# Who makes the low parts of the expert weights: every other subtraction on GpSimd, and no raw products

## The chip, the cores and the metric

The kernel runs on one NeuronCore of a Trainium2 chip, as one launch. The metric is the device time in microseconds (us), the median of several runs. The engines named below are TensorE (PE in the profile; PEld is its weight load), VectorE (DVE), ScalarE (ACT), GpSimd (POOL) and SyncE (SP, which issues most of the transfers).

## What is computed

A trunk of two layers over 256 latent tokens and 256 context tokens of width 1024: modulated norms, attention of four kinds, and in each layer a feed-forward block with 16384 experts. The change touches only that block. For a block of tokens the reference does

```
q = (xb @ wq).reshape(128, 8, 2, 128)
s = einsum('thpd,pnd->thpn', q, sub_keys)
sv, si = top_k(s, 16)
...
a = einsum('thkd,td->thk', u[eidx], xb)
wgt = gelu(a) * softmax(fv)
out = einsum('thk,thkd->td', wgt, v[eidx])
```

Each token chooses 16 of 16384 experts for each of 8 heads, from two lists of 128 keys. Layer 0 does it for 512 tokens, layer 1 for 256.

## The kernel before

Instead of gathering the chosen experts' rows, the kernel multiplies all experts for most tokens (three blocks of 128 tokens in layer 0, both blocks in layer 1; the fourth block of layer 0 is gathered). The 16384 experts are 128 chunks of 128. For a chunk i, the *first product* (`achunk`, L1032) is the chunk's 128 rows of `u` against all tokens, in PSUM; ScalarE applies Gelu and evicts it into a ring (L1046). The *second product* (`fchunk`, L1188) multiplies the gated result by the chunk's rows of `v` and is accumulated over all chunks.

Products are made to nearly full precision in a fast matmul type: an operand is split into a high part (a ScalarE cast, L169) and a low part (operand minus high part, a VectorE subtraction, L170; both in `split`, L168), and `mm3` (L191) makes three matmuls of each product: high by high (L193) and the two mixed ones (L194, L195). The names in the profile: `w` is a raw weight tile (six buffers), `ws` a split half (six buffers, so three chunks), `hh`/`hl`/`hp` the split activations. A first product of a chunk has 8 blocks of the depth, so 24 matmuls: high by high (L193), high by the activations' low part (L194), low by high (L195). In `achunk` the weight's low part is first needed by the third matmul, the call at L195.

Layer 1 has a second way: for every fifth of its first chunks (`raw(i)`, L1023: i below the lag, i % 5 == 0) the unsplit weights go against unsplit activations `h32` at the slow matmul type (`product8`, L212, matmul L215: 8 matmuls that the trace shows as 16 passes). Such a chunk needs no cast and no subtraction. `RAWQ` does the same for some blocks of layer 1's query projection and is not touched.

The stretch in question: while routing (top-16 lists, VectorE) and gates are worked out, TensorE has no second products to make, so the kernel runs ahead with first products: 27 chunks in layer 0, 47 in layer 1 (`LAG`), which lie in the ring. The order is written by the program: `prologue()` (L1059) yields after each piece of routing or gate work, and whenever its accumulated weight allows, the loop at L1082 emits the next `achunk`. In the gates (`gates`, L928) VectorE makes one-hot tables (`oh`, L954: 128x2048 fp16) and products with the gate (`og`, L957, L960), ScalarE scales a part (L964), TensorE multiplies them (L978), ScalarE evicts (L981). In layer 0 a filler also does the conditioning of later layers (`ada`, L252, with a GpSimd memset at L241).

`achunk(i)` first asks for loads of chunks i to i+3 on SP's queue (`load_u`), then for splits of i and i+1 (`split_u`, L1026), then emits the matmuls and Gelu. An instruction waits on its engine in program order: a cast of chunk i+1 needs the ws buffers of chunk i-2 to be free (its matmuls done), the subtraction needs the cast, TensorE's matmuls need both. After the lag the same `achunk` runs in the main loop, with the second products; there all splits stay on VectorE and ScalarE.

GpSimd in this kernel: the small power functions of the norms (L317), and in layer 0's main loop the copies of gather indices (L1135, L1138) and the gathers (L1141).

Of the kernel before, what the change touches and what calls it, by code (L numbers as in the profile page):

```python
# [10 lines left out]
F = mybir.dt.float32  # L11
# [5 lines left out]
OP = mybir.AluOpType  # L17
# [26 lines left out]
RSTEP = 4  # L44
U_AHEAD = (1, 3)
RAWQ = (3, 6, 9, 12, 15)
RAWU = (1, 5)
CAND = ((0, 1, 16, 0), (1, 3, 8, 16), (4, 4, 4, 40), (8, 8, 1, 56))
CAND_LO = (0, 16, 24, 32, 40, 44, 48, 52, 56, 57, 58, 59, 60, 61, 62, 63)

# [41 lines left out]
class Kernel:  # L92
# [903 lines left out]
    def peer(self, l, xs, sq, nd):  # L996

        nc = self.nc
# [3 lines left out]
        lag = LAG[l]  # L1002
# [12 lines left out]
        ustr, usp, useen, vstr, gstr, ring = {}, {}, set(), {}, {}, {}  # L1015

        def load_u(i):
            if i < NCH and i not in useen:
                useen.add(i)
                ustr[i] = self.wraw_t()  # L1020
                nc.sync.dma_start(ustr[i], A["uT"][l, i].rearrange("p k e -> p (k e)"))

        def raw(i):  # L1023
            return self.h32 is not None and i < lag and i % RAWU[1] < RAWU[0]

        def split_u(i):  # L1026
            if i < NCH and i not in usp and not raw(i):
                h, o = self.wsp_t(), self.wsp_t()
                self.split(ustr.pop(i), h, o)
                usp[i] = (h, o)  # L1030

        def achunk(i):  # L1032
            for k in range(U_AHEAD[1] + 1):
                load_u(i + k)
            for k in range(U_AHEAD[0] + 1):
                split_u(i + k)
            p = self.ps()
            if raw(i):
                self.product8(p[:, c], ustr.pop(i))
            else:  # L1040
                uh, ul = usp.pop(i)
                for k in range(8):
                    b = slice(k * 128, (k + 1) * 128)
                    self.mm3(p[:, c], uh[:, b], ul[:, b], hh[:, k, c], hl[:, k, c], k == 0, k == 7)
            ring[i] = rg.t("ring", [128, TD])
            nc.scalar.activation(ring[i], p[:, c], AF.Gelu)  # L1046

        def ahead(b):
            if b >= 14:
                load_u(b - 14)  # L1050
            if b == 17:
                split_u(0)
# [26 lines left out]
        i = 0  # L1079
        tot = (6 - EARLY[l]) * RW0[l] + 6 * (nd - 1) * RW + nd * (32 + 2 * GPIPE)  # L1080
        done = 0
        for n, w in enumerate(prologue()):  # L1082
            done += w
            if n % FSTEP == 0:
                next(filler, None)
            while i < lag and i * tot < done * (lag - TAIL[l]):
                achunk(i)
                i += 1
# [121 lines left out]
        while i < lag:  # L1210
            achunk(i)
            i += 1
        split_v(0)
        weight(0)
        for j in range(NCH):
            load_v(j + 2)
            if j + lag < NCH:
                achunk(j + lag)
            split_v(j + 1)
            weight(j + 1)  # L1220
            if lt and j < LATE:
                next(lt, None)
            elif lt:
                n1 = pace(j)
                for n in range(nu, n1):
                    use(n)
                gather(nu + NGB, n1 + NGB, wts[j + 1][:, 0, 0:1].bitcast(F) if j + 1 < NCH else None)
                nu = n1
            if j < NCH - 2:
                fchunk([j])  # L1230
# [264 lines left out]
```

## Time and profile before

| what | us |
|---|---|
| median of 3 runs (lowest, highest) | 2643.84 (2643.66, 2646.22) |
| the profiled execution, its own time | 2645.51 |
| its span, first to last instruction | 2643.7 |
| busy in the span: TensorE, VectorE, ScalarE, GpSimd | 2539.7, 1860.0, 1195.9, 529.4 |
| layer 0, routing and gates with first products | about 410 to 620 |
| layer 1, the same | about 1870 to 2050 |

How to read it: the span is what the trace covers; the time lies 1.8 us above it. Busy time of TensorE is from modelled ends of pipelined matmuls, so full does not mean at its peak. A row of a group gives line, engine, operation, output <- inputs, shape, count | busy time in us, mean ns of one | idle time of the engine before them and who ended it. In the timeline a row is start in us, duration in us, engine, line, operation. A VectorE instruction's duration overlaps the next one's start a little.

### The profile page before, as it was taken

What the parts mean: (1) busy time and instruction counts of PE and PEld (TensorE: products, weight loads), DVE (VectorE), ACT (ScalarE), POOL (GpSimd) and SP (SyncE); (2) the same over time, 40 slices, a digit from 0 to 9 for tenths busy, and PEclk for the clock granted to TensorE, in tenths of its full rate; (3) what the DMA queues carried; (4) which work ended last, traced back from release to release, by engine and by line L of the source; (5) the groups of instructions that cost most, each with busy time, mean ns of one, the idle gap of its engine ahead of it and who ended that gap; (6) DMA issues with size and microseconds to landing.
All of it is one profiled execution on the core that took longest, in us unless ns stands there. A gap on an engine that the chain in (4) does not pass through costs nothing. (4 is left out here: it accounts for less than half of the span.)

```text
span 2643.7 us, 42831 instructions
## 1 busy us (share of the span) xinstructions
PE 2539.7 (96%) x16145; PEld 2223.6 (84%) x16145; DVE 1860.0 (70%) x3870; ACT 1195.9 (45%) x2189; POOL 529.4 (20%) x516
## 2 busy tenths in 40 slices
PE   7999999989999999999999998999999999999998
PEld 5866788878899999999889777768999999999886
DVE  4377689997877777777778656477997755555555
ACT  4254336784333333333333333454587444444444
POOL 0000000000165555566665531000000000000000
PEclk9999999999999999999999998999999999999999
DMA  7371325977798888888888763464479866666355
GB/s 299 105 252 60 117 92 177 305 237 253 241 328 314 318 309 320 314 308 315 298 301 304 250 222 106 140 220 153 145 246 307 309 230 213 209 214 209 126 192 183
DMA packets 239375, 610.86 MB, mean 231 GB/s; under 512 B 18128, under 2 KB 102592, under 8 KB 239168
## 3 DMA queue, kind: packets, MB, share of 16 engines
q1 hardware_dynamic: 202304, 473.90, 52.2%
q0 software_dynamic: 36864, 134.23, 14.4%
q8 instruction: 126, 2.06, 0.3%
q14 instruction: 81, 0.66, 0.1%
HBM read 558.76 MB, written 49.31 MB: 230 GB/s over the span
## 5 line engine op out<-in xcount | busy, mean ns | idle before, releaser
L169 ACT CAST ws<-w 128x1024 fp32r<-128x1024 f32 (+1 forms) x327 | 342.1, 1047 | 639.0 <-PE p L194 589.5
L170 DVE TENSOR_TENSOR ws<-w,ws 128x1024 fp32r<-128x1024 f32 (+1 forms) x327 | 397.3, 1216 | 234.7 <-ACT ws L169 233.0
L194 PE MATMUL p<-vs,w 128*128 128x512 f32 x1280 | 503.7, 394 | 9.4 <-DVE vs L170 9.3
L169 ACT CAST vs<-v 128x1024 fp32r<-128x1024 f32 x256 | 269.6, 1053 | 525.1 <-PE p L194 515.7
L193 PE MATMUL p<-vs,w 128*128 128x512 f32 x1280 | 501.4, 392 | 4.2 <-ACT w L1182 4.2
L195 PE MATMUL p<-vs,w 128*128 128x512 f32 x1280 | 502.0, 393 | 0.0
L193 PE MATMUL p<-hh,ws 128*128 128x384 f32 (+1 forms) x1304 | 458.3, 352 | 3.2 <-DVE fu L372 1.8
L195 PE MATMUL p<-hh,ws 128*128 128x384 f32 (+1 forms) x1304 | 454.0, 348 | 1.1 <-DVE ws L170 1.1
L194 PE MATMUL p<-hl,ws 128*128 128x384 f32 (+1 forms) x1304 | 454.0, 348 | 0.1
L170 DVE TENSOR_TENSOR vs<-v,vs 128x1024 fp32r<-128x1024 f32 x256 | 312.6, 1221 | 164.8 <-ACT vs L169 164.7
L193 PE MATMUL p<-hp,ws 128*128 128x256 f32 x1032 | 295.6, 287 | 2.4 <-ACT ws L169 2.4
L195 PE MATMUL p<-hp,ws 128*128 128x256 f32 x1032 | 293.2, 284 | 0.0
L194 PE MATMUL p<-hp,ws 128*128 128x256 f32 x1032 | 293.2, 284 | 0.0
L194 PEld LDWEIGHTS p<-vs,w 128*128 128x128 f32 x1280 | 242.1, 189 | 57.6 <-DVE vs L170 11.9
L195 PEld LDWEIGHTS p<-vs,w 128*128 128x128 f32 x1280 | 241.9, 189 | 53.4 <-DVE w L1183 1.8
L193 PEld LDWEIGHTS p<-vs,w 128*128 128x128 f32 x1280 | 242.0, 189 | 50.9 <-ACT w L1182 5.2
L317 POOL TENSOR_TENSOR rso<-rsm,mhalf 128x1 f32<-128x1 f32 x30 | 20.2, 675 | 1221.7 <-DVE rsm L315 1207.2
L193 PEld LDWEIGHTS p<-hh,ws 128*128 128x128 f32 x1304 | 246.0, 189 | 19.0 <-issue 2.6
L194 PEld LDWEIGHTS p<-hl,ws 128*128 128x128 f32 x1304 | 245.8, 188 | 14.7 <-DVE hl L374 0.3
L195 PEld LDWEIGHTS p<-hh,ws 128*128 128x128 f32 x1304 | 245.4, 188 | 12.3 <-DVE ws L170 1.4
L1153 DVE SCALAR_TENSOR_TENSOR acc<-gr,ga,acc 128x1024 f32<-128x1024 f32 x128 | 164.0, 1281 | 107.6 <-DMA gr<-in_v,ix 107.1
L1148 DVE SCALAR_TENSOR_TENSOR gr<-gr,hn 128x1024 f32<-128x1024 f32 x128 | 155.9, 1223 | 99.5 <-DMA gr<-in_u,ix 99.0
(271 smaller groups left out, 3974.1 us busy)
## 6 DMA issues: line engine op xcount, KB each, us to landing
w<-in_uT SPq DMA_DIRECT2D x256, 512.0 KB
v<-in_v SPq DMA_DIRECT2D x256, 512.0 KB
w<-in_ada_w SPq DMA_DIRECT2D x96, 512.0 KB
G<-stage SPq DMA_DIRECT2D x40, 1024.0 KB
g<-G SPq DMA_DIRECT2D x32, 768.0 KB
w<-in_wq SPq DMA_DIRECT2D x32, 512.0 KB
g<-G SPq DMA_DIRECT2D x32, 512.0 KB
w<-in_w_out SPq DMA_DIRECT2D x16, 512.0 KB
```

The lines of the kernel that those rows point to most:

```text
L169: self.nc.scalar.copy(hi, raw)
L170: self.nc.vector.tensor_tensor(lo, raw, hi.bitcast(F), op=OP.subtract)
L193: m(out, lh, rh, start=start, stop=False)
L194: m(out, lh, rl, start=False, stop=False)
L195: m(out, ll, rh, start=False, stop=stop)
L317: nc.gpsimd.tensor_tensor(o, m, self.mhalf[:, :n], op=OP.pow)
L1148: nc.vector.scalar_tensor_tensor(t, t, 1.0, hn, op0=OP.mult, op1=OP.mult, accum_out=ga[:, 0, n:n + 1])
L1153: nc.vector.scalar_tensor_tensor(acc, t, ga[:, 0, n - 128:n - 127], acc, op0=OP.mult, op1=OP.add)
```

## The change

Two things. `RAWU` becomes (0, 5), so `raw(i)` is false for every chunk: layer 1's 10 raw first products become split ones. And in `split_u` the low part of a chunk i below the lag with odd i is subtracted by GpSimd in place of VectorE, after the same ScalarE cast; at odd i (up to two below the lag) `achunk` also asks for the split of i+2, one chunk further ahead than before. So splits are now asked for in pairs at odd chunks: i+1, VectorE's, and i+2, GpSimd's.

```diff
-RAWU = (1, 5)
+RAWU = (0, 5)
...
         def split_u(i):
             if i < NCH and i not in usp and not raw(i):
-                h, o = self.wsp_t(), self.wsp_t()
-                self.split(ustr.pop(i), h, o)
+                h, o, u = self.wsp_t(), self.wsp_t(), ustr.pop(i)
+                if i < lag and i % 2:
+                    nc.scalar.copy(h, u)
+                    nc.gpsimd.tensor_tensor(o, u, h.bitcast(F), op=OP.subtract)
+                else:
+                    self.split(u, h, o)
                 usp[i] = (h, o)
 
         def achunk(i):
             for k in range(U_AHEAD[1] + 1):
                 load_u(i + k)
-            for k in range(U_AHEAD[0] + 1):
+            for k in range(U_AHEAD[0] + 1 + (i < lag - 2 and i % 2)):
                 split_u(i + k)
```

## Rows read from the trace of the kernel before

**Rows 1.** The page: busy us, share of the span, instructions of each engine.
```profile
PE 2539.7 (96%) x16145; PEld 2223.6 (84%) x16145; DVE 1860.0 (70%) x3870; ACT 1195.9 (45%) x2189; POOL 529.4 (20%) x516
```
**Rows 2.** Busy time by stretch: us, then each engine, clock, DMA.
```profile
core 0: us, PE busy (x) PEld busy (x) DVE busy (x) ACT busy (x) POOL busy (x), PEclk, DMA share, GB/s
...
410.00:590.00 180.00, 160.93 (x1620) 146.97 (x1619) 172.16 (x396) 140.77 (x334) 0.21 (x1) 0.95 0.76 245
590.00:640.00 50.00, 45.79 (x261) 42.70 (x260) 32.33 (x115) 24.09 (x42) 0.00 (x0) 0.93 0.86 293
1890.00:2020.00 130.00, 127.58 (x1215) 123.32 (x1214) 121.68 (x236) 105.40 (x253) 0.00 (x0) 0.99 0.73 235
2020.00:2050.00 30.00, 30.00 (x240) 29.12 (x238) 13.41 (x18) 16.35 (x28) 0.00 (x0) 1.00 1.02 355
```
**Rows 3.** TensorE's waits from 410 to 590 us, and a slice of 10 us.
```profile
PE p L978 <- DVE og L957: 8.6, 8, 2.1
...
PE p L195 <- DVE ws L170: 1.1, 1, 1.1
...
550.00:560.00 10.00, 8.81 (x59) 8.66 (x60) 8.35 (x12) 6.17 (x16) 0.00 (x0) 0.67 0.65 202
```
**Rows 4.** TensorE's waits from 1890 to 2020 us (all), and a slice of 10 us.
```profile
PE p L193 <- ACT ws L169: 2.4, 1, 2.4
...
1930.00:1940.00 10.00, 7.60 (x57) 7.24 (x57) 9.63 (x19) 8.54 (x20) 0.00 (x0) 0.83 0.95 312
```
**Rows 5.** Groups: VectorE and evictions, 410 to 590 us; then 1890 to 2020 us.
```profile
L954 DVE TENSOR_TENSOR oh<-io,ijgt 128x2048 f16<-128x2048 f16 x47 | 57.5, 1224 | 3.6 <-ACT ijgt L936 2.7 <-PE p L978 0.9
L957 DVE TENSOR_TENSOR og<-oh,ijgt 128x1024 f16<-128x1024 f16 x47 | 32.5, 691 | 0.6
L170 DVE TENSOR_TENSOR ws<-w,ws 128x1024 fp32r<-128x1024 f32 x22 | 26.7, 1217 | 1.0 <-ACT ws L169 1.0
L960 DVE TENSOR_TENSOR og<-oh,ijgt 128x512 f16<-128x512 f16 x46 | 19.2, 418 | 0.0
...
L1046 ACT ACTIVATE ring<-p x23: 478/492/548, 409.5 to 584.7; 128x384 f32<-128x384 f32 x23
...
L170 DVE TENSOR_TENSOR ws<-w,ws 128x1024 fp32r<-128x1024 f32 x27 | 32.8, 1219 | 6.2 <-ACT ws L169 6.1
...
L1046 ACT ACTIVATE ring<-p x32: 356/378/441, 1890.4 to 2017.2; 128x256 f32<-128x256 f32 x32
```
**Rows 6.** Timeline of VectorE: a low part and the instruction behind it.
```profile
1890.30 1.22 DVE L170 TENSOR_TENSOR ws<-w,ws 128x1024 fp32r<-128x1024 f32 x1
1891.43 0.68 DVE L923 TENSOR_TENSOR e<-e 128x1024 f16<-128x1024 f16 x1
```
**Rows 7.** Small instructions by line, whole span: least, median, most ns.
```profile
L317 POOL TENSOR_TENSOR rso<-rsm,mhalf x30: 549/550/1461, 7.6 to 2638.7; 128x1 f32<-128x1 f32 x30
...
L315 DVE TENSOR_SCALAR rsm<-ss x16: 143/154/154, 7.3 to 2638.4; 128x1 f32<-128x1 f32 x16
...
L1135 POOL COPY ix<-w x108: 182/599/2829, 718.6 to 1547.4; 128x1 f32<-128x1 f32 x108
```
**Rows 8.** Timeline of TensorE: first matmul of a split, raw and split chunk.
```profile
1899.30 0.36 PE L193 MATMUL p<-hp,ws 128*128 128x256 f32 x1
...
1902.26 3.62 PE L215 MATMUL p<-h,w 128*128 128x256 f32 x16
1905.53 0.47 PE L193 MATMUL p<-hp,ws 128*128 128x256 f32 x1
```
**Rows 9.** Timeline of layer 0's gather stage: GpSimd, then VectorE.
```profile
728.78 1.24 POOL L1135 COPY ix<-w 128x1 f32<-128x1 f32 x1 [5.01 <-ACT w L1182]
730.09 1.09 POOL L1138 COPY ix<-idx 128x3 int32<-128x3 int32 x1
...
728.76 1.23 DVE L1148 SCALAR_TENSOR_TENSOR gr<-gr,hn 128x1024 f32<-128x1024 f32 x1 [2.12 <-DMA gr<-in_u,ix]
...
729.91 1.22 DVE L170 TENSOR_TENSOR ws<-w,ws 128x1024 fp32r<-128x1024 f32 x1
```
**Rows 10.** ScalarE's casts, 1890 to 2020 us, and a slice of 10 us.
```profile
L169 ACT CAST ws<-w 128x1024 fp32r<-128x1024 f32 x26 | 27.2, 1052 | 10.6 <-PE p L194 9.5 <-issue 1.0
...
2000.00:2010.00 10.00, 10.00 (x97) 9.46 (x96) 9.93 (x14) 10.00 (x26) 0.00 (x0) 1.00 0.70 212
```

## The prediction

> **What bounds the kernel now.** I began with the busy times: TensorE works 2539.7 us of a 2643.7 us span, VectorE 1860.0, ScalarE 1195.9, GpSimd 529.4 [rows 1]. That names TensorE, but as an average; the change acts only in the two stretches where expert routing, gates and the first expert products overlap. So I read stretches next, with the columns of busy time side by side. From 410 to 590 us (layer 0) VectorE is busy 172.16 of 180 us and TensorE 160.93; from 1890 to 2020 us (layer 1) VectorE 121.68 of 130 and TensorE 127.58; GpSimd does 0.21 us in the first and nothing in the second [rows 2]. The tails behind them, 590 to 640 and 2020 to 2050 us, leave VectorE idle for 17.7 and 16.6 us, so nothing is to be won or lost on VectorE there [rows 2].
>
> The waits say which of two full engines ends last. In layer 0 TensorE waits 8.6 us for one-hot products of VectorE (L957) and 1.1 us for a weight's low part, and from 550 to 560 us the granted clock, 0.67, shows it partly at the lower level, behind those waits [rows 3]. VectorE bounds that stretch. In layer 1 TensorE's only wait is 2.4 us, for a high part, with the clock at 0.83 in its slice [rows 4]: TensorE bounds, VectorE follows 6 us behind. Neither has room for more work.
>
> **The change, part by part.**
>
> *Subtractions that leave VectorE.* A low part costs VectorE 1.22 us, but a following instruction starts 1.13 us after it, so 1.13 us is what it takes from the queue [rows 5, 6]. In layer 0's stretch 23 chunks are evicted and VectorE makes 22 low parts; half, 11, go: 11 x 1.13 = 12.4 us. In layer 1's stretch 32 chunks are evicted and 27 low parts made; with the raw products gone all chunks are split, 16 stay on VectorE and 16 go to GpSimd, so 11 leave: 12.4 us again [rows 5]. Over the whole layers it is 13 fewer in each (27 to 14, 37 to 24).
>
> *Subtractions that come to GpSimd.* No row shows GpSimd at such a size. Below: not faster than VectorE, 1.22 us [rows 5]. Above: its smallest two-input instruction takes 0.55 us against 0.154 us for VectorE's of that shape [rows 7]; by that ratio 4.4 us. [...] As work on an idle engine it is hidden; its cover is that the subtraction for chunk i+2 is issued at odd i, two chunks' products (2 x 2.96 us, [rows 8]) ahead.
>
> *What it does to VectorE.* In the gather stage GpSimd copies one to three elements per partition. The one that starts at 728.78 us lasts 1.24 us and ends at 730.02, just behind a two-input VectorE instruction that ended at 729.99; the next starts at 730.09 and ends at 731.18, just behind one that ended at 731.13 [rows 9]. Undisturbed, such a copy takes 0.18 us [rows 7]. So GpSimd's read of SBUF waits out a whole VectorE instruction with two SBUF inputs. What the rows don't show is the other direction, VectorE held by a long read of GpSimd: the copies are too short. Its bounds are nothing (GpSimd always yields) and the whole subtraction. I take the whole, because the direction that is seen excludes by whole instructions, not by sharing, and because the copies do get in between VectorE instructions that follow each other without a gap, so a subtraction will too.
>
> [...]
>
> VectorE's two-input share: in layer 0 the four largest groups, all with two SBUF inputs, make 57.5 + 32.5 + 26.7 + 19.2 = 136 of 172 us [rows 2, 5], and the smaller routing products add to it. I take 0.85 of the stretch. Then layer 0: 11 x 2.26 x 0.85 = 21.1 us of blocking less 12.4 is +8.7 us on VectorE; layer 1: 16 x 2.26 x 0.85 = 30.7 less 12.4 is +18.3 us. Idle time on VectorE is 7.8 and 8.3 us [rows 2]; if all of it absorbs, +0.9 and +10.0 remain, if none, the full sums. Layer 0's idle lies in few places: I take the middle, +5. Layer 1: +12.
>
> *Raw products to split ones.* A raw chunk (16 passes, L215) holds TensorE from 1902.26 to 1905.53 us, 3.27 us; a split chunk (24 matmuls) from 1899.30 to 1902.26, 2.96 [rows 8]. 10 chunks x 0.31 = 3.1 us less on TensorE. Where VectorE bounds this only makes TensorE wait longer; the two raw chunks in the tail are worth 0.6 us.
>
> *ScalarE.* 10 more casts of 1.05 us [rows 10], and casts now come in pairs at odd chunks. Behind the second cast on ScalarE wait the Gelu of that chunk, the gate scalings and the stage evictions, and behind those TensorE's gate products. ScalarE has time except late in layer 1's stretch (10.00 of 10 us from 2000 to 2010 [rows 10]). Three of the casts fall there: 0 to 3 us, I take 1.
>
> *Transfers and other queues.* No bytes change. A raw chunk's buffer, held until its product ended, is now free after the subtraction, so SP's loads can only start earlier: nothing, hidden by chunks loaded three ahead. On GpSimd nothing else is queued in these stretches but gate memsets of layer 0 (0.21 us of work, [rows 2]), which no product waits for soon. The other stages run the same instructions.
>
> The sum: 5 + 12 + 1 - 1 = +17 us, against the profiled execution's own 2645.5 us: 2662.5. The median of the three runs, 2643.84, is 1.7 below it, so I forecast **2661 us**.
>
> **The rivals.**
>
> *VectorE is not held.* GpSimd reads only in the gaps. For it: the gather stage's VectorE instructions show no long ones beside GpSimd's copies. Against: these copies read next to nothing. Then layer 0 loses 12.4 us of VectorE work in a stretch that VectorE bounds; TensorE can recover the 8.6 + 1.1 us of waits [rows 3], most of it, say 9. Layer 1 recovers TensorE's 3.1 us and about 2 of the 2.4 us wait [rows 4]. Together -14: **2630 us**, faster. It decides if VectorE's loss per subtraction stays under 1.13 / 0.85 = 1.3 us.
>
> *A short hold.* GpSimd's subtraction takes about VectorE's own 1.22 us: 1.22 x 0.85 = 1.04 lost for each that goes. Layer 0 is 1 us better; in layer 1, 16 go for 11 saved, +4 us that idle time absorbs, and TensorE's 3.1 us come in part: **2641 us**, no change.
>
> *The low part comes late.* If a subtraction takes 4.4 us, the chain at an odd chunk is cast 1.05 twice, a wait of up to 1.2 and 4.4: 7.9 us against 5.9 us of products [rows 8, 10], and TensorE's third matmul of the chunk waits, some 2 us in each of 16 chunks, with VectorE held longer as well: 2690 us or more.
>
> That the change doesn't do what it says I can exclude for the raw products (the test is false for every chunk); an odd chunk below the lag always takes the GpSimd branch.
>
> **How the numbers follow.** My forecast, VectorE held for about 2.3 us: 0.47, and its own range is 2650 to 2684. No hold: 0.30. Short hold: 0.12. Late low parts: 0.11. What a measurement of this kernel can tell from no change is about 0.2%, 5.3 us: faster is under 2638.5, slower over 2649.1. Faster 0.30, same 0.12, slower 0.47 + 0.11 = 0.58. Since cases of both signs hold much of the chance, the range runs from just under the no-hold time, 2628, to the end of the forecast's own, 2684 (nothing absorbed, 27, a subtraction of 2.7 us adding 0.45 x 27 x 0.85 = 10, and 3 for ScalarE); it leaves out the late case and a little of the no-hold one.
>
> **What would show it.** Right: GpSimd subtractions of 2 us and more in both stretches; VectorE instructions with two SBUF inputs that start or end behind them, seen as longer durations of L954 (now 1.22 us) or as starts put off by 1 to 2 us; TensorE's waits for L957 and L954 grown in layer 1 where there are none now; the stretch up to the last early chunk longer by some 12 us in layer 1 and 5 in layer 0, all else shifted only. Wrong: VectorE durations unchanged beside GpSimd's work, and VectorE idle in the stretch grown by about 12 us in layer 0; or TensorE waiting for GpSimd directly at the third matmul (L195) of odd chunks.

## The result, and the profile after

The changed kernel takes **2674.89 us** (median of 4 runs, 2673.23 to 2677.54) against 2645.03 for the kernel before in the same comparison: a ratio of 1.011, with a 95% interval of 1.0096 to 1.0124. That is slower by 30 us. The forecast was 2661 us with a range of 2628 to 2684 and a chance of 0.58 for slower: the sign and the range held, and the loss was almost twice the one worked out.

First the page of the kernel after: its span, the busy time of each engine, and the shares of the chain that ended last.

```profile
span 2673.8 us, 43062 instructions
...
PE 2546.3 (95%) x16225; PEld 2233.0 (84%) x16225; DVE 1885.5 (71%) x3844; ACT 1205.1 (45%) x2199; POOL 613.9 (23%) x552
...
PE 30%; DVE 6%; ACT 1%; issue 1%; DMA 0%; POOL 0%; SPq 0%; DVEq 0%; POOLq 0%; ACTq 0%
```

Against [rows 1] GpSimd works 84.5 us more: its 36 subtractions take 97.5 us, and its small copies in the gather stage took some 11 us less. VectorE, from which 26 subtractions were taken, works 25.5 us **more**. On the chain that ended last VectorE's share went from 1% to 6%; this is the same line of the kernel before:

```profile
PE 35%; DVE 1%; ACT 1%; issue 0%; DMA 0%; POOL 0%; DVEq 0%; POOLq 0%; ACTq 0%
```

GpSimd's own share is 0% in both: its work is not what the end waits for.

Then the stretches of [rows 2], in the kernel after (us, then busy time of each engine, granted clock, DMA share, GB/s).

```profile
410.00:590.00 180.00, 156.43 (x1515) 143.32 (x1513) 171.02 (x381) 128.91 (x305) 32.58 (x12) 0.91 0.70 229
1890.00:2020.00 130.00, 114.61 (x1060) 111.03 (x1059) 118.62 (x231) 87.56 (x198) 36.35 (x14) 0.95 0.56 180
2020.00:2050.00 30.00, 26.33 (x267) 25.48 (x266) 28.82 (x31) 27.25 (x70) 8.03 (x3) 0.94 0.90 266
```

VectorE is about as full as before in both stretches with fewer instructions done, and TensorE has lost 4.5 and 13 us of work. From 2020 to 2050 us VectorE, which was idle for 16.6 of 30 us, is now nearly full: the stretch is still going on.

Where the time was lost can be followed by the same chunk's Gelu in both traces. The one that starts at 584.7 us in layer 0 starts at 596.4 after, 11.7 us later, and through most of layer 0's main loop the lag is 13.1 us. Between 1265 and 1420 us it falls to 7.9, and the first raw product of layer 1's query projection starts at 1834.4 us against 1824.9, so 9.5 us remain from layer 0. The fall is not the change's doing: the trace of the second experiment below, whose layer 0 is the same program as before, gains 5.4 us on the kernel before at the same place, so the kernel before lost some 5 us there in its profiled execution. From 1834 us on the lag grows to 31.4 us at chunk 40 of layer 1, ends at 30.1 at chunk 46 and stays there to the end. So the stretch of layer 0 lost 12 to 13 us, of which 9.5 are left at layer 1, and layer 1 lost 20.5 us. A split by layer from single traces like these is uncertain by a few us.

What the subtractions did is seen in the groups of the kernel after: the GpSimd subtraction over the whole span, then VectorE from 405 to 600 us (count | busy us, mean ns | idle before).

```profile
L1031 POOL TENSOR_TENSOR ws<-w,ws 128x1024 fp32r<-128x1024 f32 x36 | 97.5, 2710 | 464.2 <-ACT ws L1030 285.8 <-PE p L836 102.1 <-PE p L978 41.4
...
L954 DVE TENSOR_TENSOR oh<-io,ijgt 128x2048 f16<-128x2048 f16 x47 | 57.5, 1224 | 5.3 <-ACT ijgt L936 5.3
L957 DVE TENSOR_TENSOR og<-oh,ijgt 128x1024 f16<-128x1024 f16 x46 | 42.3, 920 | 0.7
L170 DVE TENSOR_TENSOR ws<-w,ws 128x1024 fp32r<-128x1024 f32 x10 | 14.4, 1435 | 1.2 <-ACT ws L169 1.2
```

Against [rows 5] the one-hot product L957 has a mean of 920 ns in place of 691, the low part 1435 in place of 1217. These means mix many undisturbed instructions with a few very long ones. One of the latter, first GpSimd's timeline, then VectorE's:

```profile
524.62 2.80 POOL L1031 TENSOR_TENSOR ws<-w,ws 128x1024 fp32r<-128x1024 f32 x1 [21.25 <-PE p L978]
```

```profile
524.00 1.22 DVE L954 TENSOR_TENSOR oh<-io,ijgt 128x2048 f16<-128x2048 f16 x1
525.15 2.42 DVE L906 TENSOR_TENSOR xs<-xs,sv 128x128 int32<-128x128 int32 x1
```

GpSimd starts at 524.62 and first waits until L954 ends at 525.22. Then it reads for about 2.2 us, and L906, whose own time is 0.29 us, lasts 2.42 and ends at 527.57, just behind GpSimd at 527.42. That is the direction that no row of before showed: a long GpSimd read holds VectorE for its whole length. This pattern stands 11 times in layer 0's stretch: the lengthened instructions, each against the shortest of its own line and shape, add up to 22.7 us. In layer 1 it is 30.4 us over 18 subtractions from 1885 to 2045 us, of which 3 lengthened nothing. Call such a lengthening a hold.

Last, TensorE's waits after: from 400 to 640 us the longest (the first line), then all from 1880 to 2070 us.

```profile
PE p L978 <- DVE og L957: 13.7, 11, 3.5
...
PE p L195 <- DVE ws L170: 6.8, 6, 3.3
PE p L193 <- ACT ws L169: 5.1, 2, 3.8
PE p L195 <- POOL ws L1031: 3.4, 3, 1.3
PE p L978 <- DVE og L960: 2.7, 2, 2.3
PE p L978 <- DVE og L957: 1.3, 2, 0.7
```

In layer 0 the wait of [rows 3] for L957 grew from 8.6 to 13.7 us (each of the other waits there changed by less than 3 us). In layer 1, where 2.4 us was all [rows 4], there are 19.3 us now, 10.8 of them for VectorE, 5.1 for ScalarE and only 3.4 for GpSimd itself.

### The profile page after: what moved, and what is told of

It is laid out like the page before. It is cut to its first block, busy times and chain, and to the rows that moved or that the text cites. A ratio compares the mean times of both kernels' runs of the same rounds, so it can differ in the third digit from the quotient of the medians.

```text
span 2673.8 us, 43062 instructions
## 1 busy us (share of the span) xinstructions
PE 2546.3 (95%) x16225; PEld 2233.0 (84%) x16225; DVE 1885.5 (71%) x3844; ACT 1205.1 (45%) x2199; POOL 613.9 (23%) x552
## 5 line engine op out<-in xcount | busy, mean ns | idle before, releaser
L169 ACT CAST ws<-w 128x1024 fp32r<-128x1024 f32 (+2 forms) x301 | 315.1, 1047 | 616.9 <-PE p L194 536.8
L170 DVE TENSOR_TENSOR ws<-w,ws 128x1024 fp32r<-128x1024 f32 (+2 forms) x301 | 368.2, 1223 | 242.3 <-ACT ws L169 240.8
L170 DVE TENSOR_TENSOR vs<-v,vs 128x1024 fp32r<-128x1024 f32 x256 | 313.0, 1222 | 157.7 <-ACT vs L169 151.9
L195 PE MATMUL p<-hp,ws 128*128 128x256 f32 x1112 | 318.6, 287 | 10.2 <-DVE ws L170 6.8
L193 PE MATMUL p<-hp,ws 128*128 128x256 f32 x1112 | 319.2, 288 | 5.2 <-ACT ws L169 5.1
L194 PE MATMUL p<-hp,ws 128*128 128x256 f32 x1112 | 317.0, 285 | 0.0
L1152 DVE SCALAR_TENSOR_TENSOR gr<-gr,hn 128x1024 f32<-128x1024 f32 x128 | 155.9, 1222 | 102.4 <-DMA gr<-in_u,ix 101.8
```

The lines of the kernel that those rows point to most:

```text
L169: self.nc.scalar.copy(hi, raw)
L170: self.nc.vector.tensor_tensor(lo, raw, hi.bitcast(F), op=OP.subtract)
L193: m(out, lh, rh, start=start, stop=False)
L194: m(out, lh, rl, start=False, stop=False)
L195: m(out, ll, rh, start=False, stop=stop)
L1152: nc.vector.scalar_tensor_tensor(t, t, 1.0, hn, op0=OP.mult, op1=OP.mult, accum_out=ga[:, 0, n:n + 1])
```

## The experiments

The theory: the loss comes from VectorE being held while GpSimd reads SBUF. The rivals: the raw products given up (more work for ScalarE and VectorE), the new order of splits (pairs at odd chunks), a late GpSimd result, or GpSimd's writing rather than its reading. Kernels that were compared ran beside runs of the kernel before on the same chip: 2645.17 us for the first four runs below, 2647.34 for the next two, 2645.57 for the last three.

### The subtraction back on VectorE, all else as in the change

```diff
-                    nc.gpsimd.tensor_tensor(o, u, h.bitcast(F), op=OP.subtract)
+                    nc.vector.tensor_tensor(o, u, h.bitcast(F), op=OP.subtract)
```

> The changed kernel with the same order of casts and the same look-ahead of i+2 at odd chunks, raw products gone, but every subtraction on VectorE. Theory 'hold': layer 0 within 2 us of before; layer 1 as in the kernel with only the raw products gone, 2 to 7 us: 2645 to 2653 us. Rival 'pairs' (the paired casts hold up ScalarE's queue, since the second cast waits for the product of chunk i-1): most of the 30 us stay: 2662 to 2676 us.

Measured: 2646.32 us, a ratio of 1.0005 (0.9993 to 1.0016). With one word changed, the 30 us are gone. The pairs, the longer look-ahead, the casts in twos and the raw products given up cost nothing that can be measured as long as VectorE subtracts.

### The raw products given up alone

```diff
-RAWU = (1, 5)
+RAWU = (0, 5)
```

> The kernel before with the raw first products of layer 1 as split ones, all subtractions on VectorE, no longer look-ahead. 10 more subtractions (1.13 us) and casts (1.05 us), TensorE 3.1 us less. Theory 'hold': VectorE, full in that stretch, gets 6 x 1.13 = 7 us more there and TensorE 2 us less: 2 to 7 us slower than before, 2646 to 2651 us. Rival 'raw': layer 1's whole 20 us come from here: 2660 to 2666 us.

Measured: 2647.11 us, 1.0011 (0.9999 to 1.0024). Ten more subtractions on VectorE and ten fewer raw products come out even. The table under "Why" uses its trace again.

### The raw products kept, the rest of the change as it is

```diff
-RAWU = (0, 5)
+RAWU = (1, 5)
```

> Only the subtractions move: GpSimd makes the low parts of odd chunks (13 in layer 0, 18 in layer 1), the 10 raw first products of layer 1 stay. Theory 'hold' (a GpSimd subtraction keeps VectorE's next two-input instruction out for about 2.2 us): layer 0 as in the changed kernel, 9.5 us later at the start of layer 1's block; layer 1 loses 18 x 2.2 x 0.85 = 34 us of VectorE time for 18 x 1.13 = 20 us saved, 8 us of idle time absorbing part, so 6 to 14 us; together 2660 to 2669 us. Rival 'raw' (the time of layer 1 went with the raw products, which cost VectorE and ScalarE nothing): layer 1 loses no more than 4 us, together 2653 to 2658 us.

Measured: 2665.19 us (2662.86 to 2668.17), 1.0081 (1.006 to 1.0102). In its profile layer 0 lost 9.1 us, counted as above at the start of layer 1, as in the full change, and layer 1 8.3 in place of 20.5. With the raw chunks GpSimd makes 18 low parts in layer 1 and not 23, and VectorE 19 and not 24. So the second half of the change, harmless by itself, makes the first half dearer: it brings five more holds and gives five subtractions back to VectorE, by the forecast's prices 5 x 2.26 x 0.85 + 5 x 1.13 = 15 us. The two profiles differ by 12 us there, the medians of the two kernels by 10.

### An unused subtraction added on GpSimd in layer 0

Here the kernel before keeps all its VectorE work, and GpSimd reads two operands more for each split, with nobody waiting for the result.

```diff
...
+                u = ustr.pop(i)
+                self.split(u, h, o)
+                if l == 0 and not done_[0]:
+                    scr = self.wn.t("scr", [128, 1024], R)
+                    nc.gpsimd.tensor_tensor(scr, u, h.bitcast(F), op=OP.subtract)
```

> The kernel before with a GpSimd subtraction that nobody uses after each split of layer 0's routing and gate stretch (some 24 of them, the same inputs, an output of its own); VectorE still makes all low parts. Layer 1 unchanged. Theory 'hold': 24 x 2.2 us of exclusion on VectorE, of which 0.85 falls on two-input work and some 8 us are absorbed by idle time: 33 to 48 us slower than before, 2677 to 2692 us, and as many VectorE instructions 2 us longer. Rival (GpSimd's work is free to VectorE, and the time went through the order of the splits): 0 to 4 us, 2644 to 2648 us.

Measured: 2694.84 us, 1.0196 (1.0175 to 1.0218), about 50 us slower for 25 subtractions, some 3 us over the top of what was expected. The groups of this kernel, GpSimd over the span and VectorE from 405 to 600 us:

```profile
L1035 POOL TENSOR_TENSOR scr<-w,ws 128x1024 fp32r<-128x1024 f32 x25 | 76.3, 3053 | 252.6 <-ACT ws L169 231.2 <-issue 20.1 <-DMA w<-in_uT 0.8
...
L954 DVE TENSOR_TENSOR oh<-io,ijgt 128x2048 f16<-128x2048 f16 x35 | 49.2, 1406 | 2.1 <-ACT ijgt L936 2.1
L957 DVE TENSOR_TENSOR og<-oh,ijgt 128x1024 f16<-128x1024 f16 x35 | 32.7, 936 | 0.4
L170 DVE TENSOR_TENSOR ws<-w,ws 128x1024 fp32r<-128x1024 f32 x20 | 32.5, 1631 | 0.8 <-ACT ws L169 0.8
```

The three largest VectorE groups are longer, L170 by 0.4 us on average. A subtraction that nobody needs costs about 2 us each, close to the 2.2 us of the read seen above: counted as above, 24 of the 25 held an instruction, 48.8 us in all. The expectation took off 0.15 of the holds and 8 us of idle time; little or nothing was absorbed. Late results can't be the cause here, since nothing uses them. (The unused read also holds the split's buffers longer. That could make instructions start later, but the rows show instructions that last longer.)

### Only writing: one element read, two full memsets

```diff
...
+                    scr = self.wn.t("scr", [128, 1024])
+                    nc.gpsimd.tensor_copy(scr[:, 0:1], h[:, 0:1].bitcast(F))
+                    for _ in range(2):
+                        nc.gpsimd.memset(scr, 0.0)
```

> The kernel before with, after each split of layer 0's stretch (some 24), a GpSimd copy of one element of the high part (so that it starts when the subtraction would) and two GpSimd memsets of 128x1024: GpSimd busy at the same places, but it reads next to nothing. Theory 'hold by reading': within 4 us of before, 2643 to 2649 us. Rival (any work of GpSimd beside VectorE costs it that time, or the split's buffers are held longer by another reader): half or more of what the two-input subtraction costs, 2660 us or more.

Measured: 2646.63 us, 0.9999 (0.9989 to 1.0009). The groups of this kernel, GpSimd over the span and VectorE from 405 to 600 us, and then its window of layer 0:

```profile
L1037 POOL MEMSET scr<- 128x1024 f32 x50 | 48.1, 962 | 2.9
...
L954 DVE TENSOR_TENSOR oh<-io,ijgt 128x2048 f16<-128x2048 f16 x48 | 58.7, 1222 | 4.1 <-ACT ijgt L936 2.7 <-PE p L978 1.5
L957 DVE TENSOR_TENSOR og<-oh,ijgt 128x1024 f16<-128x1024 f16 x48 | 33.1, 690 | 0.6
```

```profile
410.00:590.00 180.00, 162.01 (x1610) 148.62 (x1609) 171.73 (x415) 139.87 (x325) 74.44 (x64) 0.94 0.74 242
```

GpSimd is busy for 74 us of that stretch, more than twice the 32.6 of the change, and VectorE's instructions keep 1222 and 690 ns. Of the 74 us, 40.5 are memsets; 33.9 are the one-element copies, whose mean of about 1.6 us there is mostly waiting, as in [rows 9]: a one-element copy takes 0.18 us at its shortest [rows 7]. So a GpSimd that is busy with writing or waiting cost nothing here, though it wrote a tile twice per split. It is the reading.

### One input read instead of two

```diff
...
+                    scr = self.wn.t("scr", [128, 1024])
+                    nc.gpsimd.tensor_copy(scr, u)
```

> The kernel before with, after each split of layer 0's stretch (some 24), a GpSimd copy of the raw weights (128x1024, one input) to an output nobody uses. Theory 'hold by reading': VectorE is held for as long as GpSimd reads; with one stream in place of two some 1.1 us each, 24 x 1.1 x 0.85 = 22 us less 8 us of idle time: 12 to 24 us slower than before, 2657 to 2669 us. Rival (only two-input instructions of GpSimd exclude VectorE): under 4 us.

Measured: 2656.83 us, 1.0035 (1.0021 to 1.0049); against 2647.34 it is 9.5 us, just below the expected 12 to 24. The copy's shortest time is 1.03 us, less than half of a subtraction's. A hold by it, GpSimd and then VectorE:

```profile
508.44 3.41 POOL L1035 COPY scr<-w 128x1024 f32<-128x1024 f32 x1 [8.92 <-DMA w<-in_uT]
```

```profile
508.47 1.21 DVE L170 TENSOR_TENSOR ws<-w,ws 128x1024 fp32r<-128x1024 f32 x1
509.60 1.21 DVE L954 TENSOR_TENSOR oh<-io,ijgt 128x2048 f16<-128x2048 f16 x1
510.74 0.21 DVE L876 TENSOR_TENSOR cand<-sv 128x64 f32<-128x64 f32 x1
510.88 1.52 DVE L957 TENSOR_TENSOR og<-oh,ijgt 128x1024 f16<-128x1024 f16 x1
```

The copy was kept out while VectorE instructions with two inputs ran one behind the other, got in at about 510.8, and then L957 took 1.52 us where 0.69 is its own time: a loss of 0.83. Per instruction added, the loss is 9.5 / 25 = 0.4 us for one input and 50 / 25 = 2 us for two. It grows with the time of the read, and faster than in proportion, because the copies also hold less often: counted as above, 16 of the 25 held an instruction, for 0.87 us at most and 12.0 us in all. So the expectation was high in both of its terms, 1.1 us for a hold and 0.85 for the share that hits. Why 9 copies held nothing is open.

### The subtraction in two halves

If a hold lasts one GpSimd instruction, halves should hold twice for half as long.

```diff
+                    for x in (slice(0, 512), slice(512, 1024)):
+                        nc.gpsimd.tensor_tensor(o[:, x], u[:, x], h[:, x].bitcast(F), op=OP.subtract)
```

> The changed kernel with each GpSimd subtraction cut in two of 512 elements. Theory 'hold by reading, per instruction': each half keeps VectorE out for about 1.1 us, twice as often; the sum is the same, so within 5 us of the changed kernel, 2670 to 2681 us, and the longest VectorE instructions of the stretch are 1.1 us over their own time, not 2.2. Rival (VectorE loses a fixed time per GpSimd instruction): the cost doubles, 2695 us or more; rival (VectorE gets in between the halves, so that the stall itself, not the sum, cost the time): 2660 us or less.

Measured: 2672.14 us, 1.0098 (1.0083 to 1.0114). GpSimd's pair, then VectorE beside it, in this kernel:

```profile
455.74 3.49 POOL L1032 TENSOR_TENSOR ws<-w,ws 128x512 fp32r<-128x512 f32 x2 [8.09 <-ACT ws L1030]
```

```profile
456.29 1.78 DVE L957 TENSOR_TENSOR og<-oh,ijgt 128x1024 f16<-128x1024 f16 x1
458.00 1.51 DVE L960 TENSOR_TENSOR og<-oh,ijgt 128x512 f16<-128x512 f16 x1
```

L957 is held for 1.1 us, and L960 for 1.1 again. Here the two engines take turns by whole instructions. The sum of the holds in this trace is 21.1 us in layer 0 and 29.5 in layer 1, against 22.7 and 30.4 in the change: it stays, and so does the loss.

### Two attempts to place the subtraction where it doesn't hurt

In the top-16 lists VectorE's instructions read one input each. (A row can name two tiles, as in `sv<-sv,sc`; the trace has one input for it, the 128x128 scores, and the eight values come in ahead by a MATCH_VALUE_LOAD with a row of its own, 76 ns on average from 1825 to 1885 us in the kernel before.) So the low parts of the query weights, which are needed at that time, were given to GpSimd from block 3 on, a block ahead, in layer 1 alone or in both layers, with the expert chunks left to VectorE and no raw products.

```diff
-RAWU = (1, 5)
+RAWU = (0, 5)
...
+                if key[0] in GPW and key[1] >= 3:
+                    self.nc.scalar.copy(h, t)
+                    self.nc.gpsimd.tensor_tensor(o, t, h.bitcast(F), op=OP.subtract)
...
-        self.w_split(i + 1 + split)
+        self.w_split(i + 1 + split + (key[0] in GPW and key[1] >= 1))
```

> The kernel before, raw first products gone, all their subtractions on VectorE; but the low parts of layer 1's query weights (blocks 3 to 15 that are split, 8 of them) go to GpSimd, one block further ahead. There VectorE works almost only on top-16 lists, instructions with one input. Theory 'hold by reading against a second input': those 8 subtractions cost VectorE next to nothing and save it 9 us before the first products; with TensorE full all the while, the gain is at most its 2.4 us wait and 3.1 us of the raw products: 2639 to 2645 us, and no top-16 instruction longer. Rival (a GpSimd read holds whatever VectorE does): 8 x 1.1 us more on a full VectorE, and the raw products' loss as before: 2652 us or more.

> As the last one, with layer 0's query weights too (13 blocks). VectorE has a sixth of its time idle there and TensorE is full, so layer 0 gains only what VectorE carries over into the first products: 0 to 4 us beside the last one, 2636 to 2645 us; the rival as there, 2655 us or more.

Measured: 2646.86 us for layer 1 alone, 1.0002 (0.9992 to 1.0011), and 2644.53 for both, 1.0 (0.9989 to 1.0011). The stretch of layer 1's lists, in the kernel before and then with the move:

```profile
1820.00:1890.00 70.00, 68.95 (x490) 65.86 (x489) 66.59 (x361) 30.73 (x56) 0.00 (x0) 1.00 0.44 144
```

```profile
1820.00:1890.00 70.00, 67.88 (x502) 65.15 (x500) 57.86 (x355) 30.95 (x56) 19.03 (x8) 1.00 0.41 136
```

And from 1825 to 1885 us, a list instruction of VectorE in the kernel before and in the one with the move:

```profile
L807 DVE FIND_INDEX8 sv<-sv,sc 128x8 uint32<-128x128 f32 x32 | 8.8, 289 | 0.0
```

```profile
L812 DVE FIND_INDEX8 sv<-sv,sc 128x8 uint32<-128x128 f32 x32 | 8.8, 287 | 0.0
```

Eight subtractions cost VectorE nothing there: it is 8.7 us less busy, and a list instruction keeps its mean (287 ns; 289 before). The mechanism did what was expected, the time didn't: layer 1 alone ended 2 us above its expected range, and the move in both layers, inside its range, gained nothing measurable. TensorE is busy 67.88 of 70 us in that stretch, so VectorE's spare time can hardly buy anything there. It bought nothing behind it either: from 1885 to 2060 us TensorE waits 4.5 us for VectorE's low parts and 2.1 us for a high part in this kernel, against 2.4 us in all before. Why the time saved in the lists does not carry over was not isolated. No version was found that measurably beats the kernel before.

## Why the prediction was right, and where it was wrong

**The hold was right, in place and size.** A subtraction was priced at 2.26 us on GpSimd and 0.85 of it on VectorE, 21.1 us in layer 0 and 30.7 in layer 1. The lengthened instructions of the trace add up to 22.7 and 30.4. In layer 0 all 11 subtractions of the stretch held something, 2.07 us each on average. In layer 1 the close match is partly luck: the sum comes from 18 subtractions where 16 were counted, at 1.69 us each where 1.92 was taken. No run shows the 2.26 us, twice VectorE's step of 1.13: it was the author's estimate, and the runs showed 2.35 to 2.41 us for the subtraction where nothing disturbed it (the eight of layer 1's query weights beside the lists) and 2.2 for a full hold. The traces now show both directions: GpSimd's copy kept out, 1.24 us where 0.18 is the shortest [rows 7, 9], and L906 held, 2.42 us where 0.29 is its own time. Which engine goes first is not settled by the order of their starts: the last section has a subtraction that was kept out by instructions that started after it.

**The subtractions taken off VectorE were right**: 26 fewer.

**The step that failed is the idle time that absorbs.** The sums on VectorE were +8.7 and +18.3 us; from them the prediction took 3.7 and 6 us, because VectorE had 7.8 and 8.3 us of idle time, and called the rest +5 and +12. Measured were 20.5 in layer 1, and in layer 0 11.7 at the end of the stretch, of which 9.5 were left at layer 1: the full sums and more. The same work, from the Gelu that starts at 1885.6 us in the kernel before to the one at 2020.5, shows what became of the idle time. First the kernel before, then the raw products given up alone, then all pairs on VectorE, then the change.

```profile
1885.62:2020.51 134.89, 132.47 (x1250) 127.82 (x1248) 126.06 (x241) 107.61 (x257) 0.00 (x0) 0.99 0.72 232
```

```profile
1885.66:2021.99 136.33, 130.52 (x1314) 128.48 (x1313) 131.42 (x245) 113.03 (x262) 0.00 (x0) 0.99 0.71 227
```

```profile
1884.05:2021.40 137.35, 130.62 (x1315) 128.27 (x1314) 133.07 (x252) 114.60 (x264) 0.00 (x0) 0.99 0.73 231
```

```profile
1894.87:2050.48 155.61, 136.55 (x1294) 132.33 (x1293) 142.60 (x234) 112.47 (x264) 44.38 (x17) 0.95 0.64 200
```

VectorE's idle time is 8.8 us, then 4.9, 4.3 and **13.0**. Where VectorE got more subtractions of its own (+5.4 and +7.0 us of work), the idle time took up some two thirds of it, and the stretch grew by only 1.4 and 2.5 us. Where it was held, its busy time rose by 16.5 us and its idle time by another 4.2, which make the 20.7 us that the stretch is longer. In layer 0 the same count, the kernel before and then the change, is

```profile
409.50:584.70 175.20, 156.94 (x1569) 143.90 (x1568) 167.39 (x395) 135.96 (x322) 0.21 (x1) 0.95 0.75 243
```

```profile
409.70:596.40 186.70, 162.53 (x1567) 149.10 (x1566) 177.65 (x389) 135.21 (x321) 32.88 (x12) 0.92 0.70 228
```

which is +10.3 busy and +1.2 idle. So the idle time took up much of the work that VectorE issues in order with the rest, and none of the holds. (The comparison is not quite clean: in the two kernels without holds TensorE also had about 2 us less to do than before.) Why holds are not absorbed wasn't isolated. What the waits suggest is that a hold falls on whichever instruction is next, often a one-hot product that ScalarE and TensorE wait for, and VectorE then waits for them in turn.

**A term that was missing: the clock.** In the last of the four rows TensorE makes about as many matmuls as in the second and third and is busy 6 us longer, with a granted clock of 0.95 in place of 0.99. It is the kernel with 19 us of idle TensorE in that stretch, where the second and third have 6 and 7 and the kernel before 2. Layer 0 shows it too: 156.94 us for 1569 matmuls at 0.95, and 162.53 for 1567 at 0.92. So TensorE is busy 5 to 6 us longer in each layer for about the same matmuls. The lower clock comes with the waits in these rows, and inside the stretch too: in the kernel before, TensorE is busy 1.1 of the 5 us from 546 to 551, and the clock is 0.50 in each us from 550 to 556 and 1.00 again from 557. Where VectorE bounds the stretch some of TensorE's added time may be hidden: how much of the loss it makes was not isolated. The prediction named the clock [rows 3, 4] and put no price on it.

**The small terms.** TensorE's gain from dropping raw products and ScalarE's extra casts cannot be told from nothing: both together, with ten more subtractions on VectorE, are the run with the raw products given up alone, +2 us with an interval that reaches zero.

**The rivals.** No hold and a short hold are refuted by the 2.42 us instruction above and by the unused subtraction, which cost about 2 us each time. The late low part was there, but small: TensorE waited for GpSimd three times, 3.4 us in all, not some 2 us in each of 16 chunks. It was priced with a subtraction of 4.4 us, and it took 2.4 when it was let in. (Its chain was added up to 7.9 us; the terms given make 7.7, which changes nothing.)

## What to carry to other kernels

Work moved to an idle GpSimd wasn't free here where it read SBUF beside a VectorE full of two-input instructions: count each such read as time taken from VectorE, in this kernel 2.2 us for a 128x1024 fp32 subtraction that VectorE does in 1.13, and up to 0.87 for a copy of that size. It was free beside the one-input instructions of the top-16 lists (287 ns with it, 289 without), though not beside one-input casts (2.46 and 2.37 us, the last rows below), and where GpSimd only wrote (a ratio of 0.9999 with two memsets per split); but then it only pays if VectorE is what that stretch waits for. And do not set a hold off against idle time in the averages: idle time took up much of the added work here, and none of the holds.

## What the runs showed of the hardware that was not expected

**VectorE can keep GpSimd out for longer than one instruction.** The prediction had GpSimd getting in between any two instructions. In the kernel after, one subtraction lasted 6.48 us (GpSimd, then part of VectorE beside it):

```profile
547.46 6.48 POOL L1031 TENSOR_TENSOR ws<-w,ws 128x1024 fp32r<-128x1024 f32 x1 [20.04 <-ACT ws L1030]
```

```profile
548.24 0.69 DVE L923 TENSOR_TENSOR e<-e 128x1024 f16<-128x1024 f16 x1
...
551.45 0.29 DVE L924 TENSOR_TENSOR ijg<-e 128x128 f32<-128x128 f16 x1
551.65 2.84 DVE L957 TENSOR_TENSOR og<-oh,ijgt 128x1024 f16<-128x1024 f16 x1
```

Eight instructions with two inputs (the first started at 547.10), each starting before the one ahead had ended, kept it out until about 551.7; then it held L957 for 2.15 us. At 525.22 us, in the rows of the first section, one instruction was enough. What decides which engine is next isn't seen in these rows.

**Casts are held too.** In layer 1 two subtractions in a row held two small casts with one input each, GpSimd and then VectorE:

```profile
1895.05 4.80 POOL L1031 TENSOR_TENSOR ws<-w,ws 128x1024 fp32r<-128x1024 f32 x2 [7.29 <-ACT ws L1030]
```

```profile
1895.12 2.46 DVE L909 CAST xs<-xs 128x128 f16<-128x128 int32 x1
1897.50 2.37 DVE L910 CAST xs<-xs 128x8 f16<-128x8 f32 x1
```

A cast of 8 elements per partition took 2.37 us, by the same timeline 2.21 more than at its shortest. The prediction counted only instructions with two inputs. Why these casts were held and the one-input instructions of the lists were not was not isolated.
